# Half of the S5 rotation tables copied backwards, addends of the modulation sent whole by SP, small inputs in one transfer

## The chip, the cores and the metric

The kernel runs on one core of a Trainium2 chip. The metric is the device time of one execution in microseconds (us); lower is better. The core has five engines with a queue of their own each: TensorE (PE, matmuls; PEld is its loading of weights), VectorE (DVE), ScalarE (ACT), GpSimd (POOL) and SyncE (SP, which here only issues transfers). ACT can issue transfers too. An engine works through its queue in order; where an instruction waits, all behind it wait.

## The reference

A decoder trunk of two layers over 256 tokens of width 1024, batch 1, float32. Each layer:

1. a modulation vector of six parts from the conditioning `c`: `mod = silu(c) @ ada_w + ada_b`, 1024 x 6144, split into shift, scale and gate for the mixers and for the experts;
2. RMS norm, scale and shift, one input projection whose columns feed four causal mixers (S5, sparse attention, RG-LRU, RWKV-7); their outputs are merged with gates, projected, and added to the residual;
3. RMS norm, scale and shift, a router and 16 SwiGLU experts of which each token uses two, added to the residual.

At the end a norm. The part that the change is about most is S5, a diagonal complex recurrence:

```
lam_bar = exp(lam * step)                     # 1024 complex numbers a layer
states[t] = lam_bar * states[t-1] + bu[t]     # t = 0 .. 255
```

The kernel turns it into a real recurrence with the modulus `r = |lam_bar|`: the input of each step is rotated by the angle of that step, run through a real scan, and rotated back. For that it needs tables of `cos(n * angle)` and `sin(n * angle)` for 256 consecutive `n`. Input and output are rotated by the same table, so only differences of `n` matter, and the count may begin anywhere.

## The kernel before

**Memory.** Weights come from HBM in tiles of 128 x 2048 floats (1 MB), each one transfer that SP issues (L228, in `issue`), in the order of one list (`order`). A tile goes into one of five "ring" pages or, while `state["wide"]` is set (in the first loads and in the experts), also into one of fifteen general pages (`M`). A page is reused as soon as what it held was read; so a transfer waits for the last reader of the page before. Scratch tiles (`M.take`) come from the same fifteen pages: up to 512 floats a partition take a quarter of a page (a slot), up to 1024 two slots, more a whole page. Which slot a scratch tile gets depends on what was taken and freed before it in the source.

**Order of the work.** The framework under the kernel places the instructions of each engine by its own estimates of times, when their operands are due; so an engine's order is not the order of the source, and changes when costs or operands change. The mixers of a layer are Python generators that are advanced in turn (`rwkv`, `others` with attention, S5 and RG-LRU, `s5_tables` in layer 0), while `fill` adds gate products and the modulations that are needed later, so that PE has work between the steps of the mixers.

**The start.** ACT issues seven small transfers (cin, two of cols, pos, freq, router_b, router_w; L253 to L291), and SP the first weights. `ada(0, 0, kt)` multiplies `csil` (silu of c) with the eight tiles of `ada_w` for the first group on PE (L487); the sum and the addend `b` are added on DVE (L503), turned into columns (L510, L512), and then the normed input is scaled, shifted and split into two halves `h_hi` and `h_lo` for the exact matmuls (L600, L608, L640).

**The addend.** For each of the six groups `ada` takes a slot of 128 x 512, clears it on GpSimd (L480) and lets ACT fetch the four rows of `ada_b` into partitions 0, 32, 64 and 96 (L481). The other rows of the sum are never used.

**The tables.** `s5_tables` (L726 to L756) runs on GpSimd alone, by doubling: with the first `n` columns of cos and sin known, the next `n` follow by one complex multiplication, six instructions (L738 to L743), and the rotation by `n` is squared (L747 to L751). Eight doublings, n = 1, 2, ..., 128, for eight rows each, so that the last multiplies 8 x 128 = 1024 floats a partition in each of its six instructions. `tt`, the scratch of 1024 floats, is freed at the end. Layer 0 builds its tables beside the first mixers; layer 1's are built while the experts of layer 0 run (`beside`, at the sixth of eight pairs). Whatever takes the slots of `tt` next waits for the last instruction that used it.

**The experts.** `first(pr)` multiplies a pair's tokens with w1 and w3 (L1601), `second(pr)` turns the hidden values around on PE (L1518), copies them to a scratch tile `gT` on ACT (L1520) and multiplies them with w2 (L1623).

Of the kernel before, what the change touches and what calls it, by code (L numbers as in the profile page):

```python
# [20 lines left out]
P = 128  # L21
# [33 lines left out]
for _n, _w in MATS:  # L55
    MAT[_n] = (_o, _w)
    _o += _w
NMAT = _o


def emit(tc, I, out):
# [85 lines left out]
def _emit(ctx, tc, I, out):  # L147
# [11 lines left out]
    def ct(name, shape, dt=F32):  # L159
        return const.tile(list(shape), dt, tag=name, name=name)  # L160
# [110 lines left out]
    def row(name, n):  # L271
        return bass.AP(tensor=I[name].tensor, offset=I[name].offset, ap=[[0, P], [1, n]])

    cols = []
    for l in range(L):
        c = ct(f"cols{l}", [P, NCOL])
        nc.scalar.dma_start(c, I["cols"][l])
        cols.append(c)

    def col(l, name, i=0, n=1):  # L280
        o = COL[name][0] + i
        return cols[l][:, o:o + n]

    pos_i = ct("pos_i", [P, 2], I32)
    nc.scalar.dma_start(pos_i, I["pos"])
    freq = ct("freq", [P, 48])
    nc.scalar.dma_start(freq, row("freq", 48))
    rtb = ct("rtb", [P, NE])
    nc.scalar.dma_start(rtb, row("router_b", NE))
    rtw = ct("rtw", [P, KT, NE])  # L290
    nc.scalar.dma_start(rtw, I["router_w"])  # L291

    rel = M.take([P, P])
    G.iota(rel, pattern=[[1, P]], base=0, channel_multiplier=-1, allow_small_or_imprecise_dtypes=True)
# [179 lines left out]
    def ada(l, g, kt):  # L474


        early = (l, g) in EARLY
        if kt == 0:
            b = M.take([P, 512])
            G.memset(b, 0.0)  # L480
            nc.scalar.dma_start(b[0:P:32, :], I["ada_b"][l, g])  # L481
            part[l, g] = b, pt("acc", [P, 512]) if early else M.take([P, 2048])
        b, p = part[l, g]
        w = get(("ada", l, g, kt))
        if early:
            for j in range(4):
                state["pe"] = PE.matmul(p[32 * j:32 * j + 32, :], csil[:, kt, :], w[:, 512 * j:512 * j + 512],  # L487
                                        start=kt == 0, stop=kt == KT - 1)
        else:
            for j in range(4):  # L490
                js = slice(512 * j, 512 * j + 512)
                if kt == 0:
                    S.activation(p[:, js], w[:, js], AF.Copy, scale=csil[:, kt, 0:1])
                else:
                    V.scalar_tensor_tensor(p[:, js], w[:, js], csil[:, kt, 0:1], p[:, js], op0=OP.mult, op1=OP.add)  # L495
        done(("ada", l, g, kt))
        if kt == KT - 1:
            if not early:
                a, p = p, pt("acc", [P, 512])
                for j in range(4):  # L500
                    PE.matmul(p[32 * j:32 * j + 32, :], ones_f[:, 0:32], a[:, 512 * j:512 * j + 512], start=True, stop=True)
                M.free(a)
            V.tensor_tensor(b, p, b, OP.add)  # L503
            mod_values(l, g, b)
# [221 lines left out]
    def s5_tables(l, tabs):  # L726

        cs, sn = M.take([P, 8, T]), M.take([P, 8, T])
        tt = M.take([P, 8, P])
        G.memset(cs[:, :, 0:1], 1.0)  # L730
        G.memset(sn[:, :, 0:1], 0.0)
        ec, es = cs5[:, l], sn5[:, l]
        n = 1
        while n < T:
            t1, sh = tt[:, :, 0:n], [P, 8, n]
            ecb, esb = bc(ec[:, :, None], sh), bc(es[:, :, None], sh)
            c0, s0, c1, s1 = cs[:, :, 0:n], sn[:, :, 0:n], cs[:, :, n:2 * n], sn[:, :, n:2 * n]
            G.tensor_tensor(t1, s0, esb, OP.mult)  # L738
            G.tensor_tensor(c1, c0, ecb, OP.mult)
            G.tensor_tensor(c1, c1, t1, OP.subtract)  # L740
            G.tensor_tensor(t1, c0, esb, OP.mult)
            G.tensor_tensor(s1, s0, ecb, OP.mult)
            G.tensor_tensor(s1, s1, t1, OP.add)  # L743
            if 2 * n < T:
                e2 = sm("s5e2", [P, 2, 8])
                t2 = sm("s5t2", [P, 8])
                G.tensor_tensor(t2, es, es, OP.mult)  # L747
                G.tensor_tensor(e2[:, 0], ec, ec, OP.mult)
                G.tensor_tensor(e2[:, 0], e2[:, 0], t2, OP.subtract)
                G.tensor_tensor(t2, ec, es, OP.mult)  # L750
                G.tensor_scalar(e2[:, 1], t2, 2.0, None, op0=OP.mult)  # L751
                ec, es = e2[:, 0], e2[:, 1]
            n *= 2
            yield
        M.free(tt)
        tabs += [cs, sn]  # L756

    B2, C8 = [P, 2, T], [P, 8, 64]
# [1014 lines left out]
def layout(i):  # L1773
# [1 line left out]
    o = {}  # L1775
    o["c"] = f("c").reshape(KT, P).T
    o["x"] = f("x").reshape(T, D)
    o["pos"] = f("positions").reshape(2, P).T
    o["ada_w"] = f("ada_w").reshape(L, KT, P, 3, 2048).transpose(0, 3, 1, 2, 4)
    o["ada_b"] = f("ada_b").reshape(L, 3, 4, 512)  # L1780
    w = f("w_in")
    u, q, k, v, iq, ik, iw, rx, rg, rw = np.split(w, np.cumsum([256, 256, 256, 256, 128, 32, 4, 256, 256]), axis=-1)

# [19 lines left out]
    w3 = f("exp_w3").reshape(L, 2, NPAIR, KT, P, DE)  # L1803
    o["w13"] = np.stack([w1, w3], axis=0).transpose(1, 3, 4, 5, 2, 0, 6).reshape(L, NPAIR, KT, P, 2048)
    o["w2"] = f("exp_w2").reshape(L, 2, NPAIR, 4, P, D).transpose(0, 2, 3, 4, 1, 5).reshape(L, NPAIR, 4, P, 2048)
    o["router_w"] = f("router_w").reshape(KT, P, NE).transpose(1, 0, 2)
    o["router_b"] = f("router_b")
    o["final_g"] = f("final_norm_g")
    half = lambda n: np.float32(10000.0) ** (-np.arange(n, dtype=np.float32) / np.float32(n))
    o["freq"] = np.concatenate([half(32), half(16)]).astype(np.float32)  # L1810
    c = np.zeros((L, P, NCOL), np.float32)

    def put(name, a):
# [12 lines left out]
    for n, s in (("conv_b", "rg_conv_b"), ("rg_br", "rg_br"), ("rg_bi", "rg_bi"), ("rg_lam", "rg_lam"), ("mu", "rw_mu"),  # L1826
                 ("w0", "rw_w0"), ("a0", "rw_a0"), ("k_k", "rw_k_k"), ("k_a", "rw_k_a"), ("r_k", "rw_r_k"),
                 ("gn_w", "rw_gn_w"), ("gn_b", "rw_gn_b")):
        put(n, f(s))
    o["cols"] = c  # L1830
    mt = np.zeros((L, P, NMAT), np.float32)

    def mput(name, a):
# [33 lines left out]
```

## Time and profile before

| | |
|---|---|
| time before, median of 3 runs | 1214.31 us (1213.58 to 1215.57) |
| the profiled execution: its own time | 1220.22 us |
| its span, first to last instruction | 1218.4 us |
| granted TensorE clock, mean | 0.960 |
| PE busy | 1101.7 us, 90% |
| DVE, ACT, POOL busy | 746.6, 371.3, 230.3 us |
| moved by DMA | 329.84 MB, mean 271 GB/s |

The profile shows one execution. A row of the timeline gives the start, the length, the engine, the source line, the operation, what it writes and reads, and in brackets the idle time of the engine before it and what ended that. `x16` means that sixteen like instructions were merged into the row. SPq, ACTq, PEq are an engine's sequencer, which issues transfers and branches. A row of waits gives who waited for whom, the sum in us, how often, and the longest. A row of a table by stage gives for each stretch its length, then busy us and instruction count of PE, PEld, DVE, ACT and POOL, the granted clock of TensorE, the busy share of the DMA engines, and GB/s.

### The profile page before, as it was taken

To read this page: it belongs to the slowest core of one execution; us is meant where nothing else is said; L and a number is where in the kernel's file an instruction comes from. 1 tells how busy PE (TensorE), PEld (TensorE's weight loads), DVE (VectorE), ACT (ScalarE), POOL (GpSimd) and SP (SyncE) were. 2 spreads that over 40 slices of the span, in tenths; PEclk is the share of its full clock that TensorE was granted. 3 is DMA by queue.
4 is the path that set the end of the run, shared out by engine and by line. 5 is a ranking of instruction groups with operands and counts; after the bars stand their busy time and mean duration, and the time that the engine had idled before them with its cause. 6 is when DMAs were issued, how large, how long until landed. Compare 5 with 4: busy or idle time off the path is not lost. (4 is left out here: it accounts for less than half of the span.)

```text
span 1218.4 us, 22986 instructions
## 1 busy us (share of the span) xinstructions
PE 1101.7 (90%) x9402; PEld 712.7 (58%) x9402; DVE 746.6 (61%) x1459; ACT 371.3 (30%) x663; POOL 230.3 (19%) x306
## 2 busy tenths in 40 slices
PE   4968998988989999999888999999898999999995
PEld 1867886866976333433238888987677743343331
DVE  5899995488777322434146899967987642243325
ACT  1643532422643111111026634433254311111112
POOL 0395211044140000009100031004524000000000
PEclk8998998998999999999898999999899999999998
DMA  8724786724565799998773467843155769999883
GB/s 359 280 99 164 287 302 223 307 105 172 208 235 215 259 421 420 421 420 361 316 288 105 172 244 290 299 175 139 42 201 224 294 228 411 420 422 420 363 360 159
DMA packets 47089, 329.84 MB, mean 271 GB/s; under 512 B 5992, under 2 KB 6120, under 8 KB 7552
## 3 DMA queue, kind: packets, MB, share of 16 engines
q1 hardware_dynamic: 45776, 327.47, 69.0%
q8 instruction: 79, 1.29, 0.4%
q10 hardware_dynamic: 1200, 0.79, 0.2%
q14 instruction: 34, 0.28, 0.1%
HBM read 327.19 MB, written 1.05 MB: 269 GB/s over the span
## 5 line engine op out<-in xcount | busy, mean ns | idle before, releaser
L640 PE MATMUL acc<-h_hi,whi 128*128 128x256 f32 x720 | 212.8, 296 | 0.0
L640 PE MATMUL acc<-h_hi,wlo 128*128 128x256 f32 x720 | 206.1, 286 | 4.9 <-DVE wlo L608 4.9
L640 PE MATMUL acc<-h_lo,whi 128*128 128x256 f32 x720 | 205.1, 285 | 1.0 <-DVE h_lo L608 1.0
L607 ACT ACTIVATE whi<-ring 128x1024 fp32r<-128x1024 f32 (+2 forms) x122 | 126.0, 1034 | 206.2 <-PE acc L640 127.1
L608 DVE TENSOR_TENSOR wlo<-ring,whi 128x1024 fp32r<-128x1024 f32 (+2 forms) x122 | 153.1, 1259 | 54.8 <-ACT whi L607 50.3
L640 PEld LDWEIGHTS acc<-h_hi,whi 128*128 128x128 f32 x720 | 139.3, 194 | 17.0 <-issue 8.5
L640 PEld LDWEIGHTS acc<-h_hi,wlo 128*128 128x128 f32 x720 | 139.3, 193 | 9.0 <-DVE wlo L608 6.9
L640 PEld LDWEIGHTS acc<-h_lo,whi 128*128 128x128 f32 x720 | 139.2, 193 | 4.7 <-issue 3.0
L1601 PE MATMUL rw<-page,page 128*32 (+1 forms) x736 | 92.3, 594 | 0.0
L495 DVE SCALAR_TENSOR_TENSOR page<-ring,csil,page 128x512 f32<-128x512 f32 x112 | 83.9, 786 | 0.0
L1601 PE MATMUL acc<-page,page 128*32 128x512 f32 (+1 forms) x688 | 83.0, 609 | 0.8 <-DVE page L1545 0.6
L1573 DVE TENSOR_TENSOR page<-page,acc 128x512 f32<-128x512 f32 x64 | 42.3, 684 | 54.8 <-PE acc L1572 54.7
L1623 PE MATMUL mx<-page,page 128*32 128x512 f32 (+1 forms) x560 | 65.7, 607 | 6.1 <-ACT page L1520 6.1
L1632 DVE SCALAR_TENSOR_TENSOR page<-mx,moslw,page 128x512 f32<-128x512 f32 x32 | 24.0, 751 | 75.3 <-PE mx L1623 73.7
L1545 DVE TENSOR_SCALAR page<-mx,scale,shift 128x256 f32<-128x256 f32 x32 | 17.4, 543 | 78.5 <-PE mx L1541 78.5
L607 ACT ACTIVATE wlo<-page 128x512 fp32r<-128x512 f32 x32 | 20.2, 631 | 129.7 <-DVE page L1632 120.7
L1543 ACT ACTIVATE page<-mx,shift,scale 128x256 f32<-128x256 f32 x32 | 18.1, 564 | 126.2 <-PE mx L1541 126.2
L1623 PE MATMUL mx<-ring,page 128*32 (+1 forms) x464 | 55.4, 614 | 0.7 <-ACT page L1520 0.7
L1601 PEld LDWEIGHTS rw<-page,page 128*32 128x32 f32 x736 | 24.4, 110 | 51.7 <-issue 49.0
L1572 PE MATMUL acc<-wlo,whi 128*128 128x512 f32 x128 | 43.0, 433 | 11.1 <-PEq L1611 5.7
L1343 POOL TENSOR_TENSOR page<-page,page 128x512 f32<-128x512 f32 x22 | 33.6, 1553 | 74.8 <-DVE page L1341 73.7
L1601 PEld LDWEIGHTS acc<-page,page 128*32 128x32 f32 x688 | 20.2, 112 | 44.3 <-issue 38.0
(523 smaller groups left out, 2125.1 us busy)
## 6 DMA issues: line engine op xcount, KB each, us to landing
page<-in_w SPq DMA_DIRECT2D x124, 1024.0 KB, 11.6
ring<-in_w SPq DMA_DIRECT2D x68, 1024.0 KB, 11.2
ring<-in_ada_w SPq DMA_DIRECT2D x45, 1024.0 KB, 5.5
ring<-in_gate_w SPq DMA_DIRECT2D x32, 1024.0 KB, 5.0
ring<-in_branch_w SPq DMA_DIRECT2D x8, 1024.0 KB, 4.9
ring<-in_w_rw SPq DMA_DIRECT2D x6, 1024.0 KB, 10.4
ring<-in_w_tm SPq DMA_DIRECT2D x6, 1024.0 KB, 4.8
ring<-in_w_fm SPq DMA_DIRECT2D x6, 1024.0 KB, 4.9
```

What stands on the lines that cost most here:

```text
L495: V.scalar_tensor_tensor(p[:, js], w[:, js], csil[:, kt, 0:1], p[:, js], op0=OP.mult, op1=OP.add)
L607: S.activation(hi, a, AF.Copy)
L608: V.tensor_tensor(lo, a, hi.bitcast(F32), OP.subtract)
L640: PE.matmul(p, w, x_, **f)
L1343: G.tensor_tensor(mix[dp], mix[dp], t, OP.add)
L1543: S.activation(xg[:, kt], p, AF.Identity, scale=sc[:, kt:kt + 1], bias=sh[:, kt:kt + 1])
L1545: V.tensor_scalar(xg[:, kt], p, sc[:, kt:kt + 1], sh[:, kt:kt + 1], op0=OP.mult, op1=OP.add)
L1572: state["pe"] = PE.matmul(p, oh[:, P * a:P * a + P], y[:, fs], start=y is yh, stop=y is yl)
L1573: V.tensor_tensor(x[:, a, fs], x[:, a, fs], p, OP.add)
L1601: PE.matmul(hh[f][32 * g:32 * g + 32, :], xg[:, kt, P * i + 32 * g:P * i + 32 * g + 32], w[:, ds(offs[g] + 512 * f, 512)], start=kt == 0, ...
L1623: PE.matmul(yp[f][32 * g:32 * g + 32, :], gT[:, ft, 32 * g:32 * g + 32], w[:, ds(offs[g] + 512 * f, 512)], start=ft == 0, stop=ft == 3)
L1632: V.scalar_tensor_tensor(t, yp[f], o["w"][:, i:i + 1], gate2[:, fs], op0=OP.mult, op1=OP.mult)
```

## The change

Three things:

- **Tables.** The count starts at column 128 instead of column 0: `cs[:, :, 128]` is the angle 0. Seven doublings, n = 1 to 64, fill columns 128 to 255. The squaring after the last of them gives the rotation by 128 steps, and is written (with the sine negated) into column 0, which is step -128. Columns 1 to 127 are steps -127 to -1: the cosines are copied, the sines negated, from columns 255 down to 129, with one GpSimd instruction each and a step of -1 in what they read. `tt` has 512 floats a partition instead of 1024, and is freed before the two copies.
- **Addends.** The host pads `ada_b` to 128 rows (each row wanted is followed by 31 rows of zeros); the clearing on GpSimd goes, and SP fetches 128 x 512 floats (256 KB instead of 8 KB) with the weights' queue.
- **Small inputs.** The host lays pos, freq, router_b, router_w and both layers' cols into one array of 128 rows; ACT fetches it with one transfer instead of six. The tiles are views of it.

```diff
+    par = ct("par", [P, NPAR])
+    nc.scalar.dma_start(par, I["par"])
...
-    cols = []
-    for l in range(L):
-        c = ct(f"cols{l}", [P, NCOL])
-        nc.scalar.dma_start(c, I["cols"][l])
-        cols.append(c)
+    cols = [of(f"cols{l}") for l in range(L)]
...
-    pos_i = ct("pos_i", [P, 2], I32)
-    nc.scalar.dma_start(pos_i, I["pos"])
-    freq = ct("freq", [P, 48])
-    nc.scalar.dma_start(freq, row("freq", 48))
-    rtb = ct("rtb", [P, NE])
-    nc.scalar.dma_start(rtb, row("router_b", NE))
-    rtw = ct("rtw", [P, KT, NE])
-    nc.scalar.dma_start(rtw, I["router_w"])
+    pos_i, freq, rtb, rtw = of("pos").bitcast(I32), of("freq"), of("router_b"), of("router_w", KT)
...
             b = M.take([P, 512])
-            G.memset(b, 0.0)
-            nc.scalar.dma_start(b[0:P:32, :], I["ada_b"][l, g])
+            nc.sync.dma_start(b, I["ada_b"][l, g])
...
-        tt = M.take([P, 8, P])
-        G.memset(cs[:, :, 0:1], 1.0)
-        G.memset(sn[:, :, 0:1], 0.0)
+        tt = M.take([P, 8, 64])
+        G.memset(cs[:, :, P:P + 1], 1.0)
+        G.memset(sn[:, :, P:P + 1], 0.0)
         ec, es = cs5[:, l], sn5[:, l]
         n = 1
-        while n < T:
+        while n < P:
...
-            c0, s0, c1, s1 = cs[:, :, 0:n], sn[:, :, 0:n], cs[:, :, n:2 * n], sn[:, :, n:2 * n]
+            c0, s0, c1, s1 = cs[:, :, P:P + n], sn[:, :, P:P + n], cs[:, :, P + n:P + 2 * n], sn[:, :, P + n:P + 2 * n]
...
-            if 2 * n < T:
...
+            last = 2 * n == P
...
+            ec2, es2 = (cs[:, :, 0], sn[:, :, 0]) if last else (e2[:, 0], e2[:, 1])
+            G.tensor_tensor(t2, es, es, OP.mult)
+            G.tensor_tensor(ec2, ec, ec, OP.mult)
+            G.tensor_tensor(ec2, ec2, t2, OP.subtract)
+            G.tensor_tensor(t2, ec, es, OP.mult)
+            G.tensor_scalar(es2, t2, -2.0 if last else 2.0, None, op0=OP.mult)
...
         M.free(tt)
+        G.tensor_copy(cs[:, :, 1:P], cs[:, :, T - 1:P:-1])
+        G.tensor_scalar(sn[:, :, 1:P], sn[:, :, T - 1:P:-1], -1.0, None, op0=OP.mult)
+        yield
         tabs += [cs, sn]
...
-    o["ada_b"] = f("ada_b").reshape(L, 3, 4, 512)
+    o["ada_b"] = np.pad(f("ada_b").reshape(L, 3, 4, 1, 512), [(0, 0)] * 3 + [(0, 31), (0, 0)]).reshape(L, 3, P, 512)
```

## Rows read from the trace of the kernel before

**Rows 1.** The page, part 1: busy time, share of the span, instructions

```profile
PE 1101.7 (90%) x9402; PEld 712.7 (58%) x9402; DVE 746.6 (61%) x1459; ACT 371.3 (30%) x663; POOL 230.3 (19%) x306
```

**Rows 2.** Table by stage: us, PE, PEld, DVE, ACT, POOL busy; clock, DMA share, GB/s

```profile
70.00:105.00 35.00, 20.78 (x126) 18.29 (x126) 33.29 (x34) 11.85 (x19) 34.67 (x39) 0.82 0.26 90
560.00:595.00 35.00, 29.50 (x219) 10.30 (x215) 7.82 (x13) 2.78 (x5) 24.17 (x28) 0.90 0.80 323
```

**Rows 3.** Timeline of PE in layer 0's experts

```profile
547.88 7.05 PE L1623 MATMUL mx<-ring,page 128*32 x64
...
577.74 0.66 PE L1518 MATMUL acc<-identr,page 128*128 128x128 f32 x4
578.33 1.92 PE L1601 MATMUL acc<-page,page 128*32 x16
585.09 3.64 PE L1623 MATMUL mx<-page,page 128*32 x16 [4.83 <-ACT page L1520]
588.50 6.50 PE L1623 MATMUL mx<-ring,page 128*32 x48
```

**Rows 4.** Timeline of ACT in the same stretch

```profile
584.44 0.60 ACT L1520 ACTIVATE page<-acc 128x512 f32<-128x512 f32 x1 [13.37 <-POOL page L743]
```

**Rows 5.** Timeline of POOL in the same stretch: the end of layer 1's tables

```profile
572.36 1.29 POOL L743 TENSOR_TENSOR page<-page,page 128x512 f32<-128x512 f32 x1
...
582.07 2.34 POOL L743 TENSOR_TENSOR page<-page,page 128x1024 f32<-128x1024 f32 x1
```

**Rows 6.** Timeline of POOL, layer 0's tables: first and last instruction of n = 128

```profile
84.11 1.90 POOL L739 TENSOR_TENSOR page<-page,s5e 128x1024 f32<-128x1024 f32 x1
...
98.56 2.74 POOL L743 TENSOR_TENSOR page<-page,page 128x1024 f32<-128x1024 f32 x1
```

**Rows 7.** Timeline of DVE, layer 0: a chain of RWKV beside the tables

```profile
66.51 3.35 DVE L837 RECIPROCAL page<-page 128x512 f32<-128x512 f32 x1
...
84.25 1.78 DVE L353 SCALAR_TENSOR_TENSOR rkt<-rkt,rwn 128x8 f32<-128x8 f32 x1
...
99.02 2.83 DVE L884 TENSOR_TENSOR page<-page,page 128x512 f32<-128x512 f32 x1
...
104.87 0.69 DVE L895 TENSOR_TENSOR page<-page,rw 128x512 f32<-128x512 f32 x1 [1.09 <-PE rw L894]
```

**Rows 8.** Timeline of DVE, layer 1: the same chain

```profile
680.07 3.35 DVE L837 RECIPROCAL page<-page 128x512 f32<-128x512 f32 x1
...
694.87 0.16 DVE L353 SCALAR_TENSOR_TENSOR rkt<-rkt,rwn 128x8 f32<-128x8 f32 x1
...
702.70 0.68 DVE L895 TENSOR_TENSOR page<-page,rw 128x512 f32<-128x512 f32 x1
703.29 0.68 DVE L884 TENSOR_TENSOR page<-page 128x512 f32<-128x512 f32 x1
```

**Rows 9.** Timeline of PE, layer 0: its two long waits for that chain

```profile
91.64 1.12 PE L868 MATMUL rw<-identr,page 128*128 128x128 f32 x4 [6.96 <-DVE page L863]
...
102.79 2.05 PE L894 MATMUL rw<-page,blk 128*128 128x512 f32 x2 [4.32 <-DVE page L891]
```

**Rows 10.** Groups of POOL instructions: line, shapes, count | busy, mean ns | idle before

```profile
L480 POOL MEMSET page<- 128x512 f32 x6 | 3.2, 526 | 110.0 <-DVE h_lo L608 66.4 <-ACT page L562 17.8 <-PE acc L487 9.8
L1184 POOL TENSOR_SCALAR page<-page 128x512 f32<-128x512 f32 x2 | 3.0, 1506 | 0.2
```

**Rows 11.** Waits of SP's queue, 0 to 40 us

```profile
SPq L228 <- DMA cols<-in_cols: 2.6, 1, 2.6
```

**Rows 12.** Table by stage, columns as in rows 2

```profile
7.00:10.00 3.00, 0.00 (x0) 0.00 (x0) 0.26 (x2) 0.00 (x0) 0.00 (x0) 1.00 0.44 149
10.00:31.00 21.00, 14.71 (x85) 3.99 (x86) 17.08 (x146) 3.28 (x9) 0.67 (x2) 0.84 1.02 421
```

**Rows 13.** Timeline of DVE at the start: the first addend

```profile
30.93 0.69 DVE L503 TENSOR_TENSOR page<-acc,page 128x512 f32<-128x512 f32 x1 [2.83 <-PE acc L487]
```

**Rows 14.** Waits of ACT, 100 to 420 us

```profile
ACT whi L607 <- DMA ring<-in_gate_w: 9.1, 3, 7.0
```

More of the change, by code (lines that the diff above doesn't have):

```diff
@@ L58 @@
 NMAT = _o
+PAR = {}
+_o = 0
+for _n, _w in [("pos", 2), ("freq", 48), ("router_b", NE), ("router_w", KT * NE)] + [(f"cols{l}", NCOL) for l in range(L)]:
+    PAR[_n] = (_o, _w)
+    _o += _w
+NPAR = _o
 def emit(tc, I, out):
@@ L272, in row, with of @@
         return bass.AP(tensor=I[name].tensor, offset=I[name].offset, ap=[[0, P], [1, n]])
-    cols = []
-    for l in range(L):
-        c = ct(f"cols{l}", [P, NCOL])
-        nc.scalar.dma_start(c, I["cols"][l])
-        cols.append(c)
+    par = ct("par", [P, NPAR])
+    nc.scalar.dma_start(par, I["par"])
+    def of(name, *shape):
+        o, n = PAR[name]
+        a = par[:, o:o + n]
+        return a.rearrange("p (a b) -> p a b", a=shape[0]) if shape else a
+    cols = [of(f"cols{l}") for l in range(L)]
     def col(l, name, i=0, n=1):
@@ L743, in s5_tables @@
             G.tensor_tensor(s1, s1, t1, OP.add)
-            if 2 * n < T:
[L745 to L752, printed above, removed]
+            last = 2 * n == P
+            e2 = sm("s5e2", [P, 2, 8])
+            t2 = sm("s5t2", [P, 8])
+            ec2, es2 = (cs[:, :, 0], sn[:, :, 0]) if last else (e2[:, 0], e2[:, 1])
[4 more added lines that the diff above has]
+            G.tensor_scalar(es2, t2, -2.0 if last else 2.0, None, op0=OP.mult)
+            ec, es = ec2, es2
             n *= 2
@@ L1777, in layout @@
     o["x"] = f("x").reshape(T, D)
-    o["pos"] = f("positions").reshape(2, P).T
+    pos = np.ascontiguousarray(f("positions").reshape(2, P).T).astype(np.int32, copy=False)
     o["ada_w"] = f("ada_w").reshape(L, KT, P, 3, 2048).transpose(0, 3, 1, 2, 4)
-    o["ada_b"] = f("ada_b").reshape(L, 3, 4, 512)
+    o["ada_b"] = np.pad(f("ada_b").reshape(L, 3, 4, 1, 512), [(0, 0)] * 3 + [(0, 31), (0, 0)]).reshape(L, 3, P, 512)
     w = f("w_in")
@@ L1805, in layout @@
     o["w2"] = f("exp_w2").reshape(L, 2, NPAIR, 4, P, D).transpose(0, 2, 3, 4, 1, 5).reshape(L, NPAIR, 4, P, 2048)
-    o["router_w"] = f("router_w").reshape(KT, P, NE).transpose(1, 0, 2)
-    o["router_b"] = f("router_b")
     o["final_g"] = f("final_norm_g")
     half = lambda n: np.float32(10000.0) ** (-np.arange(n, dtype=np.float32) / np.float32(n))
-    o["freq"] = np.concatenate([half(32), half(16)]).astype(np.float32)
+    freq = np.concatenate([half(32), half(16)]).astype(np.float32)
     c = np.zeros((L, P, NCOL), np.float32)
@@ L1829, in layout @@
         put(n, f(s))
-    o["cols"] = c
+    rows = lambda a: np.broadcast_to(a[None, :], (P, len(a)))
+    o["par"] = np.concatenate([pos.view(np.float32), rows(freq), rows(f("router_b")),
+                               f("router_w").reshape(KT, P, NE).transpose(1, 0, 2).reshape(P, KT * NE)]
+                              + [c[l] for l in range(L)], axis=1)
     mt = np.zeros((L, P, NMAT), np.float32)
```

## Prediction

> **What bounds the kernel now.** I read the busy times first: PE is busy for 90% of the span, DVE for 61%, POOL for 19% [rows 1]. So POOL, on which the changed tables run, bounds nothing by its own work; a gain can only come where somebody waits for it. Hence the table by stage: two stretches show PE below its usual share while POOL is busy [rows 2]. From 70 to 105 us PE has 20.78 of 35 us, at a clock of 0.82, and DVE (33.29) and POOL (34.67) are both nearly full. From 560 to 595 us PE has 29.50 of 35 while DVE and ACT are nearly idle and POOL works 24.17. Then the timelines of these two stretches, engine by engine, and last the start, where SP's waits and the DMA table count.
>
> **The change, part by part.**
>
> *Layer 1's tables, in the experts of layer 0.* PE stands for 4.83 us before L1623 at 585.09, for a copy of ACT (L1520) [rows 3]. That copy starts at 584.44, after 13.37 us of waiting for POOL L743 [rows 4], and POOL's last L743, with 1024 floats, runs from 582.07 to 584.41 [rows 5]. L1520 and L743 share no data: ACT writes `gT` into the slot that `tt` had. After the change `tt`'s last reader is the L743 with 512 floats, which ended at 573.65 [rows 5]. The copies behind it don't read `tt`. What ACT then waits for is L1518, done at 578.40, and its 0.60 us end by 579.05, before PE is through L1601 at 580.25 [rows 3, 4]; nothing is late next, with 4.75 us (578.40 - 573.65) to spare on POOL's side. So the 4.83 us go whole. After the stall PE was slow as well: 64 matmuls of L1623 took 9.91 us (585.09 to 595.00), against 7.05 for 64 at 547.88 [rows 3], 2.86 more, in a stretch whose granted clock is 0.90 [rows 2], between the two levels of 1.2 and 2.4 GHz, after an engine that had stood. Full gain 7.69; bounds 0 (if `gT` meets another late slot, since a smaller `tt` shifts who gets which) and 7.7; I take 7.0, near the upper end, because the row names the very instruction that goes.
>
> *Layer 0's tables.* They are read only at S5, far behind, so their end matters to nobody; their company does. The chain of RWKV on DVE from L837 to L895 takes 38.36 us in layer 0 (66.51 to 104.87) and 22.63 in layer 1 (680.07 to 702.70), where POOL has no tables [rows 7, 8]. Single instructions show how: L353 on 8 floats takes 1.78 us against 0.16, L884 2.83 against 0.68, each starting within 0.5 us of a POOL instruction of n = 128 and ending at or soon after its end [rows 6 to 8]. Six such DVE instructions meet the six of n = 128, and together they are 8.9 us longer than in layer 1. PE waits for this chain twice, 6.96 and 4.32 us [rows 9], so what DVE saves there PE gets.
>
> The six go (84.11 to 101.30 us, 14.1 us of POOL [rows 6]), two copies of 8 x 127 = 1016 floats come. No row has a copy or a backward step on POOL. Bounds by its rows with fewer inputs: a clear takes 526 ns and a multiplication by a scalar 1506 ns for 512 floats [rows 10], so 1.04 or 2.99 us for 1016. For the negation I take 2.99 (the same operation), for the copy 2.0, half way: 5.0 us for both. If they hold DVE up as long as they last, 8.9 - 5.0 = 3.9 stay; if only half of that meets DVE, 6.4. I take 4.5, since POOL's rope products then also come earlier, into the same chain. Bounds: 0 (a backward step at twice the scalar's price makes 12 us of POOL, nearly what goes) and 8.9. In layer 1 the copies lie behind `tt`'s release and beside a DVE that is nearly idle [rows 2]: nothing.
>
> The Trainium skill, GPSIMD Engine Reference, section 4.1 (Engine selection), has one-input operations of GpSimd roughly at line rate. L1184 with its 1506 ns for 512 floats [rows 10] does not agree; the measurement decides. By the page's 1.2 GHz the two copies would be an estimated 1.7 us instead of 5.0, and this part would give some 3 us more.
>
> *The small inputs.* SP's fourth weight tile waited 2.6 us for `cols`, a transfer of ACT's [rows 11]; meanwhile the DMA engines ran dry: 149 GB/s from 7 to 10 us, 421 afterwards [rows 12]. At 421 these 3 us hold what took 1.06, so 1.94 us are lost, and the start is bound by the arrival of tiles: DVE's addend at 30.93 waits for PE, PE for tiles [rows 13]. With six transfers made one, that wait has nobody left to wait for; the bytes stay the same. If the new transfer is late, `csil` is late with it (DVE also reads pos and freq), yet PE has slack there until the fifth tile. Gain 1.9, bounds 0 and 1.9.
>
> *The addends.* The first now costs 262 KB at 421 GB/s, 0.6 us, ahead of or among the tiles; start together -1.3. Clears on POOL go (526 ns each [rows 10]), off any path: nothing. The five later addends are 5 x 0.62 = 3.1 us of transfer in SP's queue, where the DMA share is 0.26 to 0.80 [rows 2]; but each also waits on SP for its slot, and the weights queue behind. ACT already waits 9.1 us in all for gate tiles [rows 14]. Bounds 0 and 3.1; I take a quarter, +0.8. ACT's queue is relieved of eleven issues, but ACT bounds nothing (30% [rows 1]).
>
> *Sum.* -7.0 - 4.5 - 1.3 + 0.8 = -12.0. Against the profiled execution (1220.22 us: span 1218.4 and 1.8 around it) that makes 1208.2; the median of the runs, 1214.31, lies 5.9 below the profiled one, so 1202.3. The terms add, since behind each place PE is close to full.
>
> **The rivals.**
>
> *The DVE chain keeps its length* (the copies and the rope products hold it up as the six did): part two is 0, 1206.8. For it speaks that some of the lengthening, 15.73 - 8.9 = 6.8 us, comes from POOL instructions that stay [rows 7, 8]; against it, that 14.1 us of POOL become about 5.
>
> *The stall moves.* Another slot puts `gT`, or a neighbour, behind another late instruction: part one is 0, 1209.3. For: slots follow the order of taking. Against: POOL is free about 8 us earlier whatever the slot.
>
> *The first addend is late.* On SP it queues behind weight tiles of 2.5 us each (1.05 MB at 421 GB/s [rows 12]). Behind two tiles of the next matrix it lands 5.6 us after the last tile of the modulation, where DVE wants it some 1.2 us after that: 4.4 us lost, 1206.7; behind all four of them (the last is half a tile) 8.1, 1210.4. For: its slot comes free only after the squares of x, late. Against: in the source it stands before these tiles. The Trainium skill, DMA: Bandwidth & Descriptors, section Queues, rings and completion order, speaks for this rival: within an engine's ring descriptors are consumed in order. No run here yet shows a small transfer behind large ones on SP's queue; on ACT's it had a ring of its own.
>
> *SP is blocked (slower).* Place: SP's queue at the addends, each waiting for its slot with all weights behind it. POOL waited 17.8 and 9.8 us for two of these slots [rows 10], harmless there. If SP stands as long, less a cover of two tiles each (5.0), 17.6 us are lost: 1219.9. It decides from 14.4 us of such waiting beyond the cover (12.0 forecast, 2.4 to be told). Against: the planner issues what is due, and 110.0 us of POOL waiting were mostly idleness.
>
> *Nothing happens* (both waits are replaced by others): 1214.
>
> **How the numbers follow.** Forecast 0.46, its own range 1198 to 1206; the chain as before 0.15; the stall moved 0.14; the late addend 0.11; SP blocked 0.08; nothing 0.06. A change of 0.2%, 2.4 us, can be told from none: below 1211.9 is faster, above 1216.7 slower. Faster: 0.46 + 0.15 + 0.12 (of the stall moved) + 0.10 (of the late addend) = 0.83; same: 0.06 and the remaining 0.03 = 0.09; slower 0.08. The range of 1196 to 1212: the low end is the upper bounds (7.7 + 8.9 + 1.9 = 18.5, 1195.8), the high end leaves out the blocked queue, nothing gained and little else.
>
> **What would show it.** Part one: no wait of ACT L1520 for POOL, and PE without a gap between L1601 and L1623. Part two: L353 and L884 in layer 0 near 0.16 and 0.68 us, L837 to L895 near 33 us, POOL done with layer 0's tables some 9 us earlier in relation to their start. Start: no hole in GB/s around 8 us; L503 near 29.6 us. Addends: SP waiting less than 5 us for any slot. It is wrong if L503 waits for a transfer, if a copy takes over 6 us, or if PE's idle time moves to another wait of the same size.

## The result, and the profile after

The changed kernel takes 1226.58 us (median of 20 runs, 1217.82 to 1231.65); the kernel before, beside it on the same chip, 1215.85 us (20 runs, 1212.13 to 1227.97). The ratio, of the means, is 1.0074, with a 95% interval of 1.0051 to 1.0096: 9.0 us slower (10.7 by the medians), where 12.0 us faster had been forecast. The profiled execution took 1231.10 us (span 1229.3), 4.5 us more than the median.

The first part of the profile's page shows that the work went as planned: POOL has 204.7 us instead of 230.3 [rows 1], DVE 17 us less. PE has 10 us more, for the same 9402 matmuls; so some ran at a lower clock (mean granted clock 0.952, before 0.960).

```profile
PE 1111.4 (90%) x9402; PEld 723.9 (59%) x9402; DVE 729.5 (59%) x1459; ACT 371.0 (30%) x663; POOL 204.7 (17%) x292
```

The table by stage, columns as in [rows 2], for the same two stretches and for the start [rows 12]:

```profile
70.00:105.00 35.00, 13.86 (x101) 13.62 (x101) 19.09 (x27) 7.41 (x13) 17.72 (x30) 0.71 0.23 77
560.00:595.00 35.00, 30.94 (x246) 11.40 (x246) 11.97 (x17) 4.33 (x8) 18.55 (x31) 1.00 0.89 365
...
7.00:10.00 3.00, 0.05 (x4) 0.05 (x8) 0.92 (x8) 0.00 (x0) 0.00 (x0) 1.00 1.02 421
```

From 70 to 105 us POOL has 17.72 us of work instead of 34.67, and yet PE has only 13.86 instead of 20.78 and DVE 19.09 instead of 33.29: both stand. From 560 to 595 us PE has gained, and its clock is full. At the start the hole in GB/s is closed (421 instead of 149).

Why PE and DVE stand is in the timelines of the stretch. First DVE:

```profile
64.17 0.45 DVE L1068 TENSOR_TENSOR page<-page,sins 128x160 f32<-128x160 f32 x1
84.84 0.24 DVE L1070 TENSOR_TENSOR page<-page 128x80 f32<-128x80 f32 x1 [20.23 <-POOL page L1066]
85.00 0.42 DVE L843 TENSOR_SCALAR page<-page 128x512 f32<-128x512 f32 x1
...
85.46 3.35 DVE L844 RECIPROCAL page<-page 128x512 f32<-128x512 f32 x1
```

Then POOL, the end of layer 0's tables:

```profile
77.20 1.03 POOL L760 COPY page<-page 128x1016 f32<-128x1016 f32 x1
78.19 1.26 POOL L746 TENSOR_TENSOR page<-page,page 128x512 f32<-128x512 f32 x1
...
79.94 2.76 POOL L761 TENSOR_SCALAR page<-page 128x1016 f32<-128x1016 f32 x1
...
84.29 0.52 POOL L1066 TENSOR_TENSOR page<-page,coss 128x160 f32<-128x160 f32 x1
```

L1066 and L1068 are the two products of the rope in attention (with the cosines on POOL, with the sines on DVE), L1070 subtracts one from the other. DVE's product is done at 64.6 us. POOL's, of the same input, stands in its queue behind the tables and starts at 84.29. The changed kernel has L1070 ahead of the RWKV chain (L843, L844, ...); the kernel before had DVE's first rope product at 107.15 us, behind that chain, whose last instruction starts at 104.87 [rows 7]. So DVE stands for 20.23 us, and PE, which needs a half that DVE makes behind it (`wlo`, L611), as well:

```profile
90.46 0.58 PE L645 MATMUL acc<-wlo,h_hi 128*128 128x256 f32 x1 [20.45 <-DVE wlo L611]
```

A second queue stands in the same stretch. The waits of SP's queue (who waited for whom, us in total, times, longest):

```profile
SPq L484 <- POOL page L746: 21.8, 1, 21.8
SPq L235 <- DVE rwn L867: 16.1, 1, 16.1
```

And the timeline of SP there:

```profile
54.12 3.46 SPq L235 DMA_DIRECT2D ring<-in_w_fm  x2
79.47 0.33 SPq L484 DMA_DIRECT2D page<-in_ada_b  x1
79.90 0.38 SPq L235 DMA_DIRECT2D ring<-in_w_fm  x1
96.39 15.99 SPq L235 DMA_DIRECT2D ring<-in_ada_w  x4
```

L484 is an addend. Its tile has the slot that `tt` left, and POOL's last instruction that uses `tt` (L746, 512 floats) ends at 79.45. Till then the weights stand behind the addend: the third `w_fm` tile is issued at 79.90 (before: three tiles between 55.94 and 66.00). The tiles of `ada_w` go from 96.39 (before: from 78.89), but for them SP waits once more, 16.1 us for DVE (L867), which is late by its own wait. So here it is not the addend that holds them: with its wait gone and DVE's left (f1_hold below) they go from 96.74.

Matching the same PE instructions in both traces gives where the path lost: the changed kernel ("after") leads by 1.6 us at 66 us, is 3.3 behind at 110, 3.1 at 560, leads by 5.8 at 594, is 0.9 behind at 649 and 6.9 at 1160, and 10.9 behind at the end. The gain at 594 is the stall in the experts: it is gone as forecast, with ACT's copy (L1527, L1520 of before) free of POOL [rows 4]. The row at 595.90 is for later.

```profile
579.87 0.66 PE L1525 MATMUL acc<-identr,page 128*128 128x128 f32 x4
...
582.20 3.62 PE L1630 MATMUL mx<-page,page 128*32 x32
...
595.90 1.83 PE L1608 MATMUL rw<-ring,page 128*32 128x512 f32 x6 [4.96 <-PEq L1618]
```

### The profile page after: what moved, and what is told of

Same layout as the page of the kernel before. It is cut to its first block, busy times and chain, and to the rows that moved or that the text cites. A ratio compares the mean times of both kernels' runs of the same rounds, so it can differ in the third digit from the quotient of the medians.

```text
span 1229.3 us, 22955 instructions
## 1 busy us (share of the span) xinstructions
PE 1111.4 (90%) x9402; PEld 723.9 (59%) x9402; DVE 729.5 (59%) x1459; ACT 371.0 (30%) x663; POOL 204.7 (17%) x292
## 5 line engine op out<-in xcount | busy, mean ns | idle before, releaser
L643 PE MATMUL acc<-h_hi,wlo 128*128 128x256 f32 x720 | 210.3, 292 | 9.4 <-DVE wlo L611 9.3
L643 PE MATMUL acc<-h_hi,whi 128*128 128x256 f32 x720 | 217.1, 302 | 0.0
L643 PE MATMUL acc<-h_lo,whi 128*128 128x256 f32 x720 | 208.9, 290 | 1.7 <-DVE h_lo L611 1.7
L611 DVE TENSOR_TENSOR wlo<-ring,whi 128x1024 fp32r<-128x1024 f32 (+2 forms) x122 | 148.4, 1220 | 64.2 <-ACT whi L610 59.8
L643 PEld LDWEIGHTS acc<-h_hi,whi 128*128 128x128 f32 x720 | 142.1, 197 | 18.3 <-issue 11.4
L643 PEld LDWEIGHTS acc<-h_lo,whi 128*128 128x128 f32 x720 | 142.3, 198 | 4.8 <-issue 2.5
L1608 PE MATMUL acc<-page,page 128*32 128x512 f32 (+1 forms) x672 | 79.6, 598 | 0.7 <-DVE page L1552 0.6
L645 PE MATMUL acc<-wlo,h_hi 128*128 128x256 f32 (+1 forms) x128 | 37.6, 296 | 22.6 <-DVE wlo L611 22.6
L1630 PE MATMUL mx<-ring,page 128*32 128x512 f32 (+1 forms) x432 | 52.3, 619 | 0.7 <-ACT page L1527 0.7
L1516 DVE SCALAR_TENSOR_TENSOR page<-page,rw 128x512 f32<-128x512 f32 x8 | 5.5, 686 | 72.8 <-ACT page L1515 72.8
```

Of the source, the lines that this page charges most:

```text
L611: V.tensor_tensor(lo, a, hi.bitcast(F32), OP.subtract)
L643: PE.matmul(p, w, x_, **f)
L645: PE.matmul(p, x_, w, **f)
L1608: PE.matmul(hh[f][32 * g:32 * g + 32, :], xg[:, kt, P * i + 32 * g:P * i + 32 * g + 32], w[:, ds(offs[g] + 512 * f, 512)], start=kt == 0, ...
L1630: PE.matmul(yp[f][32 * g:32 * g + 32, :], gT[:, ft, 32 * g:32 * g + 32], w[:, ds(offs[g] + 512 * f, 512)], start=ft == 0, stop=ft == 3)
```

## The experiments

All ratios are to the kernel before, timed beside it. "A" is DVE's wait for the rope's product behind the tables, "C" is SP's wait for the slot of `tt`.

| run | edit | ratio | 95% interval |
|---|---|---|---|
| e1_tables | before + new tables | 1.0019 | 0.9993 to 1.0044 |
| e2_addend | before + addends on SP | 1.0000 | 0.9983 to 1.0018 |
| e3_small | before + small inputs in one transfer | 0.9998 | 0.9978 to 1.0019 |
| e4_rope | after, rope's product on DVE | 0.9971 | 0.9946 to 0.9996 |
| f1_hold | after, `tt` kept | 1.0043 | 1.0022 to 1.0064 |
| f2_hold_rope | after, both | 0.9897 | 0.9872 to 0.9922 |
| e5_before_rope | before, rope's product on DVE | 1.0011 | 0.9993 to 1.0029 |
| h1_before_hold_rope | before, both | 1.0003 | 0.9982 to 1.0025 |
| g1_tables_l1 | before + new tables in layer 1 | 0.9990 | 0.9972 to 1.0008 |
| h2_best_addB | f2 with the addends of before | 0.9911 | 0.9889 to 0.9933 |
| h4_best_old_l1 | f2 with layer 1's tables of before | 0.9922 | 0.9898 to 0.9946 |
| h5_best_old_l0 | f2 with layer 0's tables of before | 1.0006 | 0.9987 to 1.0025 |
| k1_before_if | before, branch moved | 1.0108 | 1.0071 to 1.0145 |
| k2_l1_if | g1, branch moved | 1.0239 | 1.0204 to 1.0275 |
| i3_if | f2, branch moved | 1.0169 | 1.0129 to 1.0208 |

### The three parts, each alone

**e1_tables.** The kernel before with `s5_tables` exchanged, as in the change's diff.

> The kernel before with the new tables alone. Theory A (order): the tables alone put the rope's subtraction on DVE ahead of the RWKV chain, and it waits for a product that POOL has queued behind the tables. Then DVE shows a single wait of 15 to 21 us for POOL in layer 0 between 60 and 90 us, the path from 60 to 110 us is about 6 us longer than in the kernel before, the stall of 4.83 us in the experts of layer 0 is gone, and the time is 0.0 to 0.7% above the kernel before. Theory B (SP's queue): the loss comes from the addends, so this kernel is as fast as forecast for the tables, 7 to 11 us faster (ratio 0.991 to 0.994).

1.0019. DVE's order changed as expected (the rope's subtraction now ahead of the chain), but the long wait that came was another. In the waits from 50 to 95 us:

```profile
DVE wlo L608 <- ACT whi L607: 25.9, 2, 25.7
...
ACT whi L607 <- POOL s5t L748: 22.9, 1, 22.9
...
PE acc L642 <- ACT whi L607: 19.8, 1, 19.8
```

The addend is still ACT's here, cleared by POOL. The clear (L480) stands behind the tables and runs at 82.55 us, ACT issues its transfer at 83.11, and ACT's queue stands with it. So here it is ACT that stands behind the end of the tables, instead of SP. Whether by `tt`'s slot, as in the changed kernel, or only by the clear's place in POOL's queue, this run does not show. The expectation was right in the time, wrong in the engine.

**e2_addend.**

```diff
-            G.memset(b, 0.0)
-            nc.scalar.dma_start(b[0:P:32, :], I["ada_b"][l, g])
+            nc.sync.dma_start(b, I["ada_b"][l, g])
```

> The kernel before with the padded addends sent by SP alone. Theory A: DVE keeps its order of before, with no wait for POOL over 5 us in the first 110 us; the time moves by the price of the queue alone, 0 to 3 us slower (ratio 1.000 to 1.0025). Theory B: this part carries the loss, so 8 to 14 us slower (1.007 to 1.012), with SP standing at the addends and weights landing late behind them.

1.0000: on SP the addends cost nothing that can be measured, as long as nobody's late slot is theirs. Theory B falls.

**e3_small.** The one array `par` instead of six transfers, as in the change's diff.

> The kernel before with the small inputs in one transfer alone. Both theories: the dip in GB/s between 7 and 10 us is gone, SP's waits for cols, freq and router_b go, the end of the start (the first split of the scaled input) comes 1.5 to 2.7 us earlier, and the time is 1 to 3 us below the kernel before (ratio 0.9975 to 0.999) if nothing later gives it back; 1.000 if it does.

0.9998. The trace has the start 2.5 us earlier than in the kernel before at 36 us; in the time the part can't be told from nothing (interval -2.7 to +2.3 us).

Only the first of the three changes DVE's order, and the three together are worse than their sum (1.0017).

### The two waits

**e4_rope.** The changed kernel, with one word altered in `dsa`:

```diff
-                G.tensor_tensor(ma.rearrange("p h s d -> p (h s) d"), zf,
+                (V if l == 0 else G).tensor_tensor(ma.rearrange("p h s d -> p (h s) d"), zf,
```

> The changed kernel with one line altered: in layer 0 the rope's product with the cosines runs on DVE instead of POOL (2.3 us more work for DVE). Theory A: the 20.23 us wait of DVE goes; of it about 6.4 us (the offset at 72 to 109 us) come back, less at most 1.3 us for the products that now stand ahead of the RWKV chain, so 4 to 7 us faster than the changed kernel, a ratio of 1.001 to 1.005 to the kernel before. Theory B: no more than 1 us, ratio 1.006 to 1.008.

0.9971, faster than the kernel before; 12.5 us from one word (0.0103 of 1216), twice what was expected. DVE's 20.23 us are gone. SP's wait has grown instead, and PE has a wait left, for weights that come late. The waits of SP and the timeline of PE:

```profile
SPq L484 <- POOL page L746: 29.3, 1, 29.3
```

```profile
98.86 0.58 PE L643 MATMUL acc<-h_hi,whi 128*128 128x256 f32 x1 [8.78 <-ACT whi L610]
```

ACT, for which PE waits there, had itself stood 10.88 us at L496 for a tile of `ada_w` that SP had issued late.

**f1_hold.** The changed kernel, `tt` of layer 0 given back only when the mixers are through, so that no other tile gets its slot:

```diff
-        M.free(tt)
+        held.append(tt) if l == 0 else M.free(tt)
...
         mixers.close()
+        while held:
+            M.free(held.pop())
```

> The changed kernel, but the scratch of layer 0's tables is kept until the mixers of layer 0 are through, so that no other tile gets its slot. SP's wait of 21.8 us for POOL before the third addend should go. Theory A (DVE's order alone costs): DVE still waits about 20 us for the rope's product behind the tables, and the loss stays: ratio to the kernel before 1.005 to 1.008. Theory C (SP standing at the addend is the loss, DVE's wait only lies beside it): the weights behind the addend land 12 us and more earlier, and 5 us or more come back: ratio 0.999 to 1.003.

1.0043, between the two expectations. SP no longer waits for POOL (the three `w_fm` tiles go out from 54.21 to 64.37 us), DVE does:

```profile
DVE page L1072 <- POOL page L1068: 20.6, 1, 20.6
```

So taking C away alone gives 3.8 us back (0.0031 of 1216; each of the two ratios has 2.7 us to either side, so that is hardly clear of noise), and A keeps the rest: while DVE stands, SP's wait lies beside it.

**f2_hold_rope.** Both edits.

> Both: the scratch kept, and the rope's product with the cosines in layer 0 on DVE. Neither DVE nor SP has anything left that waits for POOL's tables. Theory C as an addition to A: against the run with the rope's product on DVE alone (ratio 0.9971, where SP stood 29.3 us and PE 8.78 us at 98.9 us) another 3 to 8 us go: ratio 0.991 to 0.995. Theory A alone: PE's 8.78 us were only another shape of the same chain, no gain: 0.996 to 0.998.

0.9897: 1203.80 us (6 runs, 1201.17 to 1208.52) beside 1216.37. The two waits together cost 21.5 us (1.0074 less 0.9897), and without them the change gives 12.5, about the sum of the prediction (12.0). The four kernels make a square:

| | slot of `tt` open to others | `tt` kept |
|---|---|---|
| rope's product on POOL | 1.0074 | 1.0043 |
| rope's product on DVE | 0.9971 | 0.9897 |

**e5_before_rope** and **h1_before_hold_rope**: the same edits in the kernel before.

> A control: the kernel before with the rope's product with the cosines in layer 0 on DVE. Theory A: in the kernel before nothing of DVE waits for POOL behind the tables (the rope stands behind the RWKV chain there), so the move is worth nothing by itself, at most its 2.3 us of DVE: ratio 0.999 to 1.002. If the move itself were a gain, 0.995 or less, the gain of the run with the rope's product on DVE would not speak for theory A.

> A control: the kernel before, with the same two edits as the run of both (scratch of layer 0's tables kept, rope's product with the cosines in layer 0 on DVE), none of the change. If the 12.5 us of that run are the change's own, once its two new waits are gone, this one stays at 0.999 to 1.003. If the two edits carry the gain by themselves, 0.990 to 0.994.

1.0011 and 1.0003: by themselves the edits are worth nothing that these runs can tell. They matter only where the change has put a wait.

The traces of after and of f2 fit this closely. Up to 65.7 us their PE instructions end within 0.07 us of each other; at 164 us f2 leads by 15.5 us, at 209 us by 19.8, at 1175 us by 20.7. The step between 164 and 209 us is the clock, and it is not the change's. In both PE waits for the column of a modulation (L513), 2.23 and 2.22 us. In after the granted clock then is 0.50, the lower level of 1.2 GHz, for 8 us; in f2 it stays at 1.00, the upper one. The kernel before has the same wait (L510, 2.15 us before 193.82) and 0.50 behind it. After, f2, then before:

```profile
193.00:197.00 4.00, 1.76 (x15) 1.58 (x14) 3.06 (x4) 2.17 (x4) 0.59 (x2) 0.96 0.31 127
197.00:201.00 4.00, 4.00 (x18) 2.23 (x20) 0.54 (x3) 0.00 (x0) 0.00 (x0) 0.50 0.02 6
201.00:205.00 4.00, 4.00 (x17) 1.75 (x14) 0.84 (x2) 0.66 (x2) 0.00 (x0) 0.50 0.83 274
```

```profile
178.00:182.00 4.00, 1.78 (x17) 1.72 (x16) 3.06 (x4) 2.04 (x4) 0.00 (x0) 1.00 0.44 178
182.00:186.00 4.00, 4.00 (x31) 1.97 (x31) 1.38 (x5) 0.94 (x3) 0.00 (x0) 1.00 0.37 82
```

```profile
197.00:201.00 4.00, 4.00 (x16) 0.99 (x19) 0.88 (x4) 0.66 (x2) 0.00 (x0) 0.50 0.24 43
```

Eight of the seventeen profiles have a wait of more than 1 us at this place. In seven of them the mean clock of the 8 us behind it is 0.57 to 0.79; f2 is the one with 1.00.

### What each part is worth once the waits are gone

**h2_best_addB.** f2 with the addends as before (the diff of e2 turned round).

> The run of both edits (ratio 0.9897) with the addends as in the kernel before: cleared on POOL, four rows by ACT. By the prediction's term the addends on SP cost 0.8 us (0 to 3.1) and gain 0.6 at the start, so nothing measurable: 0.988 to 0.991. If ACT or POOL stands at an addend instead (as ACT did for 22.9 us in the run with the tables alone), 0.993 or more.

0.9911, not to be told from f2: the addends on SP neither give nor take anything that these runs can tell (some 4 us to either side).

**h5_best_old_l0.** f2 with the old `s5_tables` called for layer 0 (its `tt` of 1024 floats kept as well).

```diff
-        chains = [rwkv(l, m, brs), others(l, m, tabs, brs)] + ([] if tabs else [s5_tables(l, tabs)])
+        chains = [rwkv(l, m, brs), others(l, m, tabs, brs)] + ([] if tabs else [s5_tables0(l, tabs)])
```

> The run of both edits (ratio 0.9897) with layer 0's tables as in the kernel before (twice the work on POOL beside DVE's chain). By the prediction's term 4.5 us lost, bounds 0 and 8.9: 0.9934, from 0.9897 to 0.997. If the shorter company of POOL is worth nothing to DVE, 0.9897; the chain from L837 to L895 would be as long as with the new tables.

1.0006: layer 0's tables are worth 13.3 us (0.0109 of 1217, some 4 us to either side), three times the term of 4.5 and above its bound of 8.9. The chain on DVE with the old tables (h5), and what POOL does beside two of its instructions:

```profile
66.15 3.35 DVE L879 RECIPROCAL page<-page 128x512 f32<-128x512 f32 x1
...
83.38 1.82 DVE L357 SCALAR_TENSOR_TENSOR rkt<-rkt,rwn 128x8 f32<-128x8 f32 x1
...
96.78 2.48 DVE L917 TENSOR_TENSOR page<-page,page 128x512 f32<-128x512 f32 x1
...
103.82 0.69 DVE L937 TENSOR_TENSOR page<-page,rw 128x512 f32<-128x512 f32 x1
```

```profile
83.28 1.89 POOL L744 TENSOR_TENSOR page<-page,s5e 128x1024 f32<-128x1024 f32 x1
...
96.32 2.38 POOL L748 TENSOR_TENSOR page<-page,page 128x1024 f32<-128x1024 f32 x1
```

The same chain with the new tables (f2), and POOL's two copies beside it:

```profile
65.27 3.35 DVE L846 RECIPROCAL page<-page 128x512 f32<-128x512 f32 x1
...
83.81 0.99 DVE L359 SCALAR_TENSOR_TENSOR rky<-rkt,rki 128x8 f32<-128x8 f32 x1
...
88.81 0.99 DVE L356 TENSOR_TENSOR rkt<-rky 128x8 f32<-128x8 f32 x1
89.72 1.21 DVE L611 TENSOR_TENSOR wlo<-ring,whi 128x1024 fp32r<-128x1024 f32 x1
...
94.96 0.69 DVE L904 TENSOR_TENSOR page<-page,rw 128x512 f32<-128x512 f32 x1 [0.97 <-PE rw L903]
```

```profile
83.56 1.22 POOL L762 COPY page<-page 128x1016 f32<-128x1016 f32 x1
...
88.23 3.28 POOL L763 TENSOR_SCALAR page<-page 128x1016 f32<-128x1016 f32 x1
```

37.67 us (66.15 to 103.82) against 29.69 (65.27 to 94.96): 8.0 less. With the old tables a DVE instruction that starts under one of POOL's six of 1024 floats ends with it in four cases (L357 at 85.20, POOL at 85.17), and 0.6 and 1.1 us behind it in the other two. In sum DVE's instructions take 15.9 us more than the shortest of their kind between 64 and 105 us in h5, and 7.3 between 64 and 99 in f2, 8.5 less. The two copies last 4.5 us, but hold up only one DVE instruction each, by 0.8 us (0.99 for 0.16); L611 at 89.72 runs beside the negation in its usual 1.21. PE's wait for that chain (7.11 us before 93.48 in h5, with the clock at 0.65 in the 8 us behind it) has no counterpart in f2. That is 8 of the 13 us; the rest comes later and in small steps (f2's lead over h5 is 1.1 us at 66 us, 9.1 at 118, 10.7 at 127, 12.6 at 576, 13.9 at 1178), and was not followed further.

**h4_best_old_l1** and **g1_tables_l1.** f2 with the old tables (`s5_tables1`) in layer 1, and the kernel before with the new tables in layer 1 alone. The diff is the first one's:

```diff
-        rs = experts(l, x, oh, sid, wts, used, regi, gate2, s5_tables(l + 1, tables[l + 1]) if l + 1 < L else ())
+        rs = experts(l, x, oh, sid, wts, used, regi, gate2, s5_tables1(l + 1, tables[l + 1]) if l + 1 < L else ())
```

> The run of both edits (ratio 0.9897) with layer 1's tables as in the kernel before. By the prediction's term 7.0 us lost: 0.9955. By what the profiles showed (7.3 at the stall, 2 to 5.4 of it given back before the next layer) and the run with layer 1's tables alone (1.2 us): 1 to 5 us lost, 0.9905 to 0.994.

> The kernel before, with the new tables for layer 1 alone (those in the experts of layer 0); layer 0's as before. By the prediction 7.0 us less, ratio 0.994. By what the runs with the new tables show (7.3 us gained at the stall, some 2.6 of them given back at the end of the experts) 4 to 5 us less, ratio 0.996 to 0.997. If the gain is given back whole: 0.999 to 1.001.

3.0 us (0.9922 less 0.9897, some 4 us to either side) and 1.2 us (interval -1.0 to 3.4), of 7.0 forecast; neither is clear of zero. At the stall itself the traces bear out the full gain of 7.69: between 581 and 594 us of the kernel before all eight traces with the new tables in layer 1 (and the branch in its place) gain 7.88 us. But by 649 us they have lost 3.5 to 7.1 us of it. The timeline of PE in g1 shows where:

```profile
580.85 1.92 PE L1637 MATMUL rw<-page,page 128*32 x16
588.38 2.90 PE L1608 MATMUL acc<-wlo,whi 128*128 128x512 f32 x6 [5.61 <-PEq L1647]
591.21 2.44 PE L1637 MATMUL rw<-ring,page 128*32 x16
...
604.47 0.33 PE L1554 MATMUL acc<-identr,page 128*128 128x128 f32 x1 [1.44 <-DVE page L1546]
...
615.34 1.42 PE L1608 MATMUL acc<-wlo,whi 128*128 128x512 f32 x4 [1.02 <-ACT wlo L607]
```

L1647 is the branch for overflowing experts. In the kernel before PE reached it behind all w1 and w3 matmuls of the last pair and stood 3.94 us; with the new tables it stands among them, and two waits for DVE and ACT follow (1.44 and 1.02 us, in all eight traces) that the kernel before didn't have. Where the branch takes 3.4 to 3.9 us, 3.5 to 6.1 us of the gain go; where it takes 4.9 to 5.6 us, 6.7 to 7.1.

**k1_before_if, k2_l1_if, i3_if.** An attempt to take the branch out of the way:

```diff
-            if pr == NPAIR - 1:
+            if pr == 3:
                 ov = nc.values_load(...)
```

> The kernel before, with the branch for overflowing experts (L1611) taken after the fourth pair of experts instead of the eighth, ahead of layer 1's tables. It is the base for the next run. PE's wait of 3.94 us at the branch moves to about 500 us, into a stretch where PE and DMA are both nearly full; the stall of 4.83 us before L1623 stays. Ratio 0.997 to 1.002.

> The same with layer 1's tables new. Theory B1 (the branch gives part one's gain back: with the new tables it falls into the middle of the last pair's matmuls and stops PE there): with the branch out of the way the gain of 7.3 us stays up to the next layer, 5 to 7 us less than the run with the branch moved alone, a difference of 0.004 to 0.006 in the ratio. Theory B2 (it is given back elsewhere at the end of the experts, by the weights or by DVE and ACT between the last matmuls): 1 to 3 us less, 0.001 to 0.0025.

> The changed kernel with the scratch kept and the rope's product on DVE (ratio 0.9897), and the branch taken after the fourth pair as well. Theory B1: another 3 to 5 us less, 0.9855 to 0.987. Theory B2: 0.988 to 0.991.

1.0108, 1.0239, 1.0169: all much slower, none as expected. Around 490 us, where the branch now is, DMA moves 421 GB/s and PE has no slack, so its 3.42 us stay lost (table by stage, k1, then the kernel before):

```profile
480.00:500.00 20.00, 15.59 (x118) 6.46 (x110) 7.64 (x14) 2.63 (x5) 0.00 (x0) 0.91 1.01 421
```

```profile
480.00:500.00 20.00, 19.96 (x170) 8.37 (x164) 10.37 (x21) 3.51 (x6) 0.00 (x0) 1.00 1.01 419
```

And in k2 the pattern of the two waits comes a third time. The timeline of DVE:

```profile
582.35 1.63 DVE L1586 TENSOR_SCALAR page<-slots,mosp,mowu 128x256 f32<-128x256 bf16 x2 [13.27 <-POOL page L775]
```

POOL's L775 is the last instruction that reads `tt` (581.01 to 582.31). Now a tile of the gather has its slot, DVE waits for it, and PE waits 11.91 us for DVE. In k1, with the old tables, it is SP that waits 13.0 us for POOL's L743. Since the moved branch met these new waits, the times can't tell the two theories about what gives the gain back apart. But the timeline of PE in k1 settles a part:

```profile
608.54 0.33 PE L1518 MATMUL acc<-identr,page 128*128 128x128 f32 x1 [1.44 <-DVE page L1510]
...
619.46 2.07 PE L1572 MATMUL acc<-wlo,whi 128*128 128x512 f32 x4 [1.01 <-ACT wlo L607]
```

These are the two waits that followed the branch in g1. In k1 the tables are the old ones and the branch is 120 us away, but the stall before L1623 is gone, since SP took the late slot. So these 2.5 us of what is given back come where the stall is gone, with the branch near or far, as theory B2 has it. How much the branch's new place adds stays open: it takes 0.6 us less to 1.7 us more than in the kernel before, and the clock behind it differs.

## Why the prediction was wrong

**The step that failed** is in part two: "They are read only at S5, far behind, so their end matters to nobody; their company does." Nobody reads the tables early, but three others stood behind their end, in POOL's queue and in `tt`'s slot: POOL's own rope product (and through it DVE), the next owner of `tt`'s slot (SP with an addend; in e1 ACT, behind a clear on POOL), and all that these queues hold behind them. DVE stood 20.23 us and SP 21.8, and without both waits the kernel is 21.5 us faster (f2). In the kernel before the order of DVE kept the first away from the path, and the third addend had a slot of the rope's (its clear waits 7.7 us for DVE L1064, not for POOL's tables). The prediction's own sign came true: PE's idle time moved to another wait, 20.45 us before L645. The new tables are shorter, and with them DVE's order moved the rope ahead (e1 shows the move, e2 and e3 don't). POOL was not ready for it: it was busy with the tables up to 84.29 us. That the planner counted on an earlier end is what the order suggests; its estimates are in no trace.

**The second step** is "each also waits on SP for its slot ... I take a quarter, +0.8", with its argument against the blocked queue, "the planner issues what is due". The rival *SP is blocked* came true in its mechanism: 21.8 us for one slot, or 16.8 beyond its cover of 5.0, above its bound of 14.4, though for another slot than the two that it named. It was given 0.08, and priced alone and too high: the 29.3 us of e4 cost 9.0. Not foreseen was that two queues would stand at once, each hidden by the other: C costs 3.8 us with A in place (hardly clear of noise) and 9.0 without it (0.0074 of 1216).

The steps one by one:

- *Layer 1's tables, -7.0.* Mechanism right, the stall of 4.83 us gone, 7.88 us gained there. The term was mis-sized for what follows: 3.5 to 7.1 us are given back within 55 us, at the branch, in the clock behind it and in two new waits (2.5 us); timed 1.2 and 3.0 (with 2 and 4 us to each side). "Nothing is late next" was checked for the instruction behind the stall only.
- *Layer 0's tables, -4.5.* The company of POOL is as read: 8.0 us of DVE's chain, close to the upper bound of 8.9; timed 13.3, of which 8 are followed to this chain and the rest is open. (The 8.9 itself was read 1.1 us too low: in layer 1 L880 was held up as well, 1.26 us beside POOL's rope product, for 0.17 in the changed kernel.) The working "if they hold DVE up as long as they last" was wrong: the copies last 4.5 us and hold it up for 1.7. The negation's duration was nearly right (2.76 us for 2.99; 3.28 in f2, beside a busy DVE), the copy took half (1.03 for 2.0; 1.22 in f2). The Trainium skill, GPSIMD Engine Reference, section 4.1 (Engine selection), has one-input operations near line rate: 1016 floats in 1.03 us agree, the multiplication by a scalar with 2.76 us does not.
- *Small inputs, -1.3 with the first addend.* L506 (L503 of before [rows 13]) starts at 28.19 instead of 30.93, 2.7 earlier, more than forecast; the first addend was not late. In the time 1 or 2 us can't be seen beside intervals of this width.
- *Addends on SP, +0.8.* 0.0 (e2), and h2 no different from f2.
- *The sum.* 12.0 forecast, 12.5 measured in f2. It came out by luck, in compensation: less from layer 1, more from layer 0. The split is rough: taken back one by one the parts make 13.3, 3.0 and 1.7 us, more than the whole.
- *The rivals.* The chain did not keep its length, the first addend was not late, the stall did not move in the changed kernel (in k2 it did).

What stays open: of the 24.5 us between the profiles of after and f2 at the last matmuls of the experts, 15.5 are layer 0's waits, but 4.3 are the clock step around 197 us and 3.8 lie at layer 1's branch (3.07 us of waiting and a clock of 0.63 in the 8 us behind it, against 1.81 us and 1.00). Both profiles have a wait there. The first of these two is no loss of the change, since the kernel before has that wait and that clock as well; f2's profile was spared it, and whether by its order or by chance, one profile can't say. The second goes with the fetch of instructions at the branch (last section): in after two transfers overlap there, of 1.4 and 2.4 us, in f2 it is one of 1.1.

## What to carry to other kernels

When an engine's work gets shorter, ask not only who reads its result but who stands behind it: the next instruction in its queue, and the next owner of each buffer it holds. A scratch tile's slot is a hidden dependency: give it back where its next owner is known, or keep it; here that and one word on who computes a product turned 9.0 us of loss into 12.5 of gain. And where one wait hides another, take both away before judging either.

## What the runs showed of the hardware

- Reading backwards shows no extra cost on GpSimd: a copy of 1016 floats in 1.03 us goes at the rate of a clear (0.53 us for 512 [rows 10]), and a negation of 1016 in 2.76 at no more than the rate of a multiplication forwards (1.51 us for 512). No run has a copy forwards on GpSimd to set beside it.
- In these traces a one-input instruction on GpSimd holds DVE up less than a two-input one: 0.8 us of a copy of 1.22 and of a negation of 3.28 (one case each), against 1.6 to 2.1 of each two-input one of 1.9 to 2.4. The Trainium skill, GPSIMD Engine Reference, section 8 (Key points), says that GpSimd shares its SBUF interfaces with VectorE, with contention for DVE instructions with two inputs from SBUF or in a 2-port performance mode. The rows agree for the first: L357 and L917, held up for long, have two such inputs. But a DVE copy with one input is held up as well (the kernel before, beside L738 of n = 128, then in layer 1 without tables); whether it ran in such a mode no trace shows:

```profile
89.50 2.08 DVE L863 COPY page<-rwrn 128x512 f32<-128x512 f32 x1
...
697.51 0.43 DVE L863 COPY page<-rwrn 128x512 f32<-128x512 f32 x1
```

- The branch for overflowing experts, whose block no profile shows entered, costs PE 1.4 to 5.6 us each time, and in 20 of 34 cases (two in each of the 17 profiles) a granted clock of 0.50 to 0.82 in the 8 us behind it. The Trainium skill, Runtime: NRT & Kernel Launch, section Instruction fetch mechanics, says that a branch out of the prefetched window makes the sequencer fetch instructions by DMA before it goes on. The traces bear that out: in all 34 waits a DMA packet of 16 KB of the kind "instruction" ends 1.6 to 2.3 us before PE goes on, and where the packet comes late the wait is long. The DMA queues in the wait of layer 0 of the kernel before (packets, MB, share):

```profile
q8 instruction: 1, 0.02, 1.5%
```
